# Hybrid encoder layer: the attention from the last query tile to the first with the mask written into the bias rows, and three pieces of work placed anew

## Chip, core and metric

The kernel runs on one core of a Trainium2 chip. The metric is the device time of one execution in microseconds (us). Engines are named as in the profile: PE (TensorE), DVE (VectorE), ACT (ScalarE), POOL (GpSimd), SP (SyncE, which here only issues DMAs).

## What is computed

One layer of a streaming encoder on x of 1024 tokens by 1024, in float32, with 256 memory tokens. Cut to what matters:

```python
proj = rms_norm(x, mix_pre_g) @ w_in                  # u (512) | q, k, v (8 heads x 64) | f_logit (8)
y_ssm = s5_mixer(u, ...)                              # complex diagonal SSM, gelu, gated linear unit
# forgetting attention, by query blocks of 128:
s = einsum(q_blk, k[:k_end]) * scale
s = where(q_pos >= k_pos, s + cum_log_f[q] - cum_log_f[k], -1e30)
y_fox = softmax(s) @ v[:k_end]
x = x + rms_norm(concat(rms_norm(y_ssm), rms_norm(y_fox)) @ w_out)
x = x + rms_norm(memory_cross_attention(rms_norm(x), mem_n, wq, wkv, wo))   # 4 heads
x = x + rms_norm((silu(h @ w_gate) * (h @ w_up)) @ w_down)                  # h = rms_norm(x), 2816 hidden
```

## The kernel before

**Number format.** Nearly every product is made of three matmuls (`mm3`, lines 122 to 124): each operand is split into a high and a low part (`split`: ACT writes the high part, L113, and DVE the rest, L115), and high x high, high x low and low x high are summed in PSUM.

**Stages.** In this order, by the times of the profiled execution: the input projection with the SSM (to about 232 us; its output product and gelu, L647 to L649, at 188 to 220); the forgetting attention, whose gaps PE fills with projections of the branch behind it (232 to 474); the output projection with the first value weights of the cross-attention between its products (474 to 545); the cross-attention (to 772); the FFN's gate and up products (772 to 1183); its down product (to the end).

**What sets the order.** The program is written as generators that are interleaved, and a scheduler with a cost table of its own then sets the order of every engine; `tc.high_priority` and `tc.issue_after` bend it. Tiles come from pools: 16 slabs of 8 KB a partition (`slab`), tags of smaller tiles (a 2 buffers, b 2, c 3, d 1, e 1, t2 3, yt 2), 3 split weight slabs (`whl`), 4 PSUM banks (`g`) and 2 score tiles of two banks each (`s`). A tile that is to be written waits until the last reader of its buffer is done.

**SSM output.** T holds the Toeplitz part in four quarters, for two halves s_ and two pairs of blocks. The first quarter lies in tile e; before, three more in two slabs, loaded by SP from T_d (L636). `ssm_out` makes, per half, four blocks of eight matmuls in a PSUM bank each, and ACT puts each through the gelu (L649, with one load of the activation table ahead). L318 is ACT's evacuation of the value projection, stored to v_d by POOL (L321); L299 and L300 are POOL's stores of q and k to qk_d.

**Attention.** For each of 8 heads and 8 query tiles of 128, `scores(h, t)` makes q k^T for the (t+1) x 128 keys up to the diagonal in a score tile s (L735, L736; and L738, a product of an identity and a triangle of large values that is added to the diagonal block). DVE adds the head's decay row ncb, broadcast to 128 partitions, and takes the minimum (L742; the signs are turned), ACT takes the exponential (L744), DVE scales (L745, L746). `turn` transposes the result on PE (L763) into slabs `pts`; `values` multiplies pairs of tiles with v (L777). Scores run two tiles ahead of `turn`. `prepare(h)` loads q, k and ncb of a head; it is called one head ahead. At the end `token_sums` adds up squares on PE by one-column matmuls (L239).

**Value weights.** `value_weights(h)` loads a head's values from kv_d (L1052), splits them into vh and vl, and multiplies them with wo (tiles t2 as weights against `whl`); heads 0 and 1 are stepped through between the output projection's products (`step(between)`), heads 2 and 3 follow.

**FFN.** Gate and up are done for pairs of hidden tiles by a scheme of seven products in place of eight (`gate_up`, `sums`; L1313 is every matmul of it, L1334 an addition of a bank to a kept tile, u2 one of these). `hid_sums(i)` makes four sums of a finished pair on DVE (L1371) and stores them (L1361, POOL). `wd_sums(k)` makes sums of the down weights on POOL (L1386) and stores them.

## Time and profile before

| | |
|---|---|
| median of 3 runs | 1402.24 us (1399.69 to 1403.91) |
| the profiled execution | 1403.55 us, span 1401.8 us, mean granted clock 0.996 |
| PE busy | 1373.7 us, 7149 matmuls |
| DVE, ACT, POOL busy | 973.7, 646.2, 377.3 us |
| moved by DMA | 242.03 MB, 173 GB/s in the mean |

How the lines read: a group is *line engine operation out<-in xcount | busy, mean ns | idle before it, releaser*; a timeline row is *start, duration, engine line operation out<-in xcount [idle before <-releaser]*; a wait is *engine, tile, line <- what it waited for: us in total, times, longest*. Matmuls are pipelined, so that the distance from one start to the next, not the duration, is what a matmul costs.

### The profile page before, as it was taken

The page shows a single profiled execution, that of the slowest core. Times are in us where ns is not written, and L with a number is a line of the kernel's source. Part 1 is how long each engine was busy: PE and PEld are TensorE (multiplying, and loading weights), DVE is VectorE, ACT ScalarE, POOL GpSimd, SP SyncE. Part 2 cuts the span into 40 slices and gives each one's busy share as a digit, 9 for nine tenths or more (in the row PEclk, how much of TensorE's full clock was granted, in tenths as well). Part 3 has the DMA queues.
Part 4 walks back from the last instruction along what each step waited for, and adds up shares of the span by engine and source line. Part 5 has one row for each costly group of instructions (what it writes and reads, how often), then busy time and mean ns, then how long its engine had stood idle before and what let it go on. Part 6 is the DMA issues. An engine that isn't in the chain of part 4 may idle for free.

```text
span 1401.8 us, 19885 instructions
## 1 busy us (share of the span) xinstructions
PE 1373.7 (98%) x7149; PEld 1144.9 (82%) x7149; DVE 973.7 (69%) x1740; ACT 646.2 (46%) x1262; POOL 377.3 (27%) x430
## 2 busy tenths in 40 slices
PE   9999999999999999999999999999999999999997
PEld 7889888879978777888888778888888888888886
DVE  7959954858667678445567998787777676655566
ACT  7373345866456547433344533333333334544441
POOL 0011110001111142001111466687666651000021
PEclk9999999999999999999999999999999999999999
DMA  6435765358662865035366354555444447965544
GB/s 218 141 105 165 216 222 139 83 155 252 184 194 83 222 194 186 0 105 169 131 219 233 135 180 157 189 188 173 160 141 163 153 151 245 355 195 195 180 166 165
DMA packets 104626, 242.03 MB, mean 173 GB/s; under 512 B 11528, under 2 KB 40200, under 8 KB 104336
## 3 DMA queue, kind: packets, MB, share of 16 engines
q1 hardware_dynamic: 86000, 178.86, 40.8%
q0 software_dynamic: 18528, 61.91, 12.4%
q8 instruction: 56, 0.92, 0.3%
q14 instruction: 42, 0.34, 0.1%
HBM read 172.05 MB, written 79.43 MB: 179 GB/s over the span
## 4 chain that ended last, share of the span: by engine, by line
PE 57%; DVE 2%; issue 1%; DMA 1%; POOL 0%; ACT 0%; DVEq 0%; SPq 0%; POOLq 0%; ACTq 0%
PE x L1313 15%; PE g L1313 12%; PE x L1591 7%; PE g L1591 7%; PE g L124 2%; PE g L122 2%; PE g L123 2%; PE x L122 2%; PE x L123 2%; PE x L124 2%; PE g L1109 1%; DVE op L115 1%; PE g L1220 0%; DVE ev L1371 0%; DMA slab<-in_w_gate 0%
## 5 line engine op out<-in xcount | busy, mean ns | idle before, releaser
L1313 PE MATMUL x<-slab,op 128*128 128x512 f32 x984 | 233.4, 389 | 0.0
L1313 PEld LDWEIGHTS x<-slab,op 128*128 128x128 f32 x984 | 184.7, 188 | 38.7 <-DVE op L115 0.5
L1313 PE MATMUL g<-slab,op 128*128 128x512 f32 x756 | 182.2, 390 | 2.3 <-DVE ev L1334 2.0
L115 DVE TENSOR_TENSOR slab<-slab 128x1024 fp32r<-128x1024 f32 (+2 forms) x96 | 115.0, 1208 | 82.9 <-ACT slab L113 81.2
L1313 PEld LDWEIGHTS g<-slab,op 128*128 128x128 f32 x756 | 141.6, 188 | 32.9 <-DVE ev L1334 2.4
L122 PE MATMUL g<-slab,whl 128*128 128x512 f32 (+1 forms) x416 | 151.7, 365 | 0.8 <-ACT slab L487 0.4
L123 PE MATMUL g<-slab,whl 128*128 128x512 f32 (+1 forms) x416 | 148.4, 357 | 0.0
L124 PE MATMUL g<-slab,whl 128*128 128x512 f32 (+1 forms) x416 | 148.4, 357 | 0.0
L113 ACT ACTIVATE slab<-slab 128x1024 fp32r<-128x1024 f32 (+2 forms) x96 | 99.0, 1037 | 102.4 <-DMA slab<-hs_d 75.2
L1591 PE MATMUL g<-slab 128*128 128x512 f32 x462 | 126.6, 389 | 0.0
L1591 PE MATMUL x<-slab 128*128 128x512 f32 x462 | 126.6, 389 | 0.0
L115 DVE TENSOR_TENSOR op<-slab,op 128x512 fp32r<-128x512 f32 x82 | 99.4, 1222 | 11.9 <-ACT op L113 11.5
L1591 PEld LDWEIGHTS g<-slab 128*128 128x128 f32 x462 | 86.7, 188 | 18.0
L1591 PEld LDWEIGHTS x<-slab 128*128 128x128 f32 x462 | 86.7, 188 | 18.0
L1386 POOL TENSOR_TENSOR wt<-wt 128x256 f32<-128x256 f32 x88 | 85.7, 974 | 30.6 <-DMA wt<-in_w_down 27.3
L113 ACT ACTIVATE op<-ss 128x512 fp32r<-128x512 f32 x63 | 39.5, 629 | 106.7 <-PE g L1313 50.9
L122 PEld LDWEIGHTS g<-slab,whl 128*128 128x128 f32 x416 | 78.7, 189 | 12.2 <-ACT whl L113 0.6
L124 PEld LDWEIGHTS g<-slab,whl 128*128 128x128 f32 x416 | 78.5, 189 | 11.6 <-DVE whl L115 0.2
L123 PEld LDWEIGHTS g<-slab,whl 128*128 128x128 f32 x416 | 78.7, 189 | 10.6
L113 ACT ACTIVATE op<-slab 128x512 fp32r<-128x512 f32 x82 | 51.1, 627 | 78.4 <-PE x L1313 40.8
L115 DVE TENSOR_TENSOR whl<-raw,whl 128x1024 fp32r<-128x1024 f32 (+2 forms) x58 | 66.0, 1144 | 20.8 <-ACT whl L113 20.5
L1416 POOL TENSOR_TENSOR ss<-slab 128x512 f32<-128x512 f32 x40 | 60.8, 1520 | 62.7 <-DMA slab<-in_w_gate 22.2
(397 smaller groups left out, 2876.2 us busy)
## 6 DMA issues: line engine op xcount, KB each, us to landing
hs_d<-ev POOLq DMA_DIRECT2D x77, 256.0 KB, 2.6
slab<-hs_d SPq DMA_DIRECT2D x35, 512.0 KB, 3.9
slab<-in_w_up SPq DMA_DIRECT2D x22, 512.0 KB, 4.4
wt<-in_w_down SPq DMA_DIRECT2D x44, 256.0 KB, 3.3
wt_d<-wt POOLq DMA_DIRECT2D x22, 512.0 KB, 3.8
slab<-in_w_gate SPq DMA_DIRECT2D x20, 512.0 KB
slab<-wt_d SPq DMA_DIRECT2D x20, 512.0 KB, 8.6
wd_d<-in_w_down SPq DMA_DIRECT2D x33, 256.0 KB, 4.7
```

The source lines that it names most:

```text
L113: first = act.activation(out=hi, in_=src, func=AF.Copy, scale=1.0 if mul is None else mul)
L115: (lo_eng or dve).tensor_tensor(out=lo, in0=src, in1=hi.bitcast(F32), op=ALU.subtract)
L122: pe.matmul(ps, lh, rh, start=first, stop=False)
L123: pe.matmul(ps, lh, rl, start=False, stop=False)
L124: pe.matmul(ps, ll, rh, start=False, stop=last)
L1109: pe.transpose(tp[:, k], src[:, (k0 + k) * P:(k0 + k + 1) * P], ident)
L1313: pe.matmul(ps, x[:, k], y[:, k], start=first and k + n == 0, stop=k == 3 and n == 2, skip_group_check=not first)
L1386: pool.tensor_tensor(out=o, in0=x, in1=y, op=ALU.subtract)
L1416: made[0] = pool.tensor_tensor(out=o, in0=x, in1=y, op=fn)
L1591: pe.matmul(banks[n][j], xo[:, u, js], wo[:, v], start=ends[0] and k == 0, stop=ends[1] and k == 2, skip_group_check=onto is not None)
```

## The change

The kernel is changed in four places.

1. The mask. The bf16 identity and triangle and their 64 matmuls go. `causal(h, t)` is new: POOL writes the large value in place into the diagonal block of the head's ncb tile. Since a tile's masked block must be plain for all later tiles, the query tiles of a head run from 7 to 0; each L742 of tile t is followed by `causal(h, t - 1)`, and `prepare` ends with `causal(h, 7)`. Slabs, value products, loads and the next head's `prepare` take the matching places.
2. T's two slabs become one slab and a tile of tag d, for the last quarter.
3. The split values of head 2 lie in one tile of tag a rather than two of t2; one empty step is put between heads 0 and 1.
4. `hid_sums(0)` is called behind u2 of the next `gate_up`, and each `wd_sums` from the second on one step later.

```diff
-    identb = const.tile([P, P], BF16, name="identb")
-    dve.tensor_copy(identb, ident)
-    maskb = const.tile([P, P], BF16, name="maskb")
-    pool.memset(maskb, 0.0)
-    pool.affine_select(out=maskb, in_=maskb, pattern=[[-1, P]], compare_op=ALU.is_ge,
-                       fill=-NEG, base=0, channel_multiplier=1)
...
-        full = [None] + [slab([P, 16, P], F32) for _ in range(2)]
-        T = [[tq, full[1][:, 0:8]], [full[2][:, 0:8], full[2][:, 8:16]]]
+        mid, tl = slab([P, 16, P], F32), tt("d", [P, 8, P])
+        T = [[tq, mid[:, 0:8]], [mid[:, 8:16], tl]]
...
+            causal(h, NT - 1)
+
+        def causal(h, t):
+            c = heads[h][2][:, t * P:(t + 1) * P]
+            pool.affine_select(out=c, in_=c, pattern=[[-1, P]], compare_op=ALU.is_ge, fill=-NEG,
+                               base=0, channel_multiplier=1)
...
-                dg = c1 == ke
                 pe.matmul(ps[:, c0:c1], qt, ka[:, 0, c0:c1], start=True, stop=False)
-                pe.matmul(ps[:, c0:c1], qt, ka[:, 1, c0:c1], start=False, stop=not dg)
-                if dg:
-                    pe.matmul(ps[:, ke - P:ke], identb, maskb, start=False, stop=True)
+                pe.matmul(ps[:, c0:c1], qt, ka[:, 1, c0:c1], start=False, stop=True)
...
                                      scalar=3e38, op0=ALU.add, op1=ALU.min, accum_out=nm)
+            if t:
+                causal(h, t - 1)
...
-            if t in (0, 2, 6):
+            if t in (3, 5, 7):
                 p = slab([P, 8, 256], F32)
-                if t == 0:
+                if t == 5:
...
-            if qc == 0:
+            if qc == 3:
                 yf.append(slab([P, 2, S]))
...
-        seq = [(h, t) for h in range(NH) for t in range(NT)]
+        seq = [(h, t) for h in range(NH) for t in reversed(range(NT))]
...
-                if t == 1 and h + 1 < NH:
+                if t == 6 and h + 1 < NH:
                     prepare(h + 1)
-                if (h, t) == (3, 5):
+                if (h, t) == (3, 2):
                     load_v(1)
...
-                if t % 2 and h % 2:
+                if t % 2 == 0 and h % 2:
                     values(h // 2, t // 2)
...
     def value_weights(h):
-        vh, vl = t2t([P, 2, 256], F32R), t2t([P, 2, 256], F32R)
+        if h == 2:
+            both = tt("a", [P, 2, 2, 256], F32R)
+            vh, vl = both[:, 0], both[:, 1]
+        else:
+            vh, vl = t2t([P, 2, 256], F32R), t2t([P, 2, 256], F32R)
...
     def first_values():
-        for h in range(2):
-            yield from value_weights(h)
+        yield from value_weights(0)
+        yield
+        yield from value_weights(1)
...
-    def gate_up(i, m, w, q):
+    def gate_up(i, m, w, q, behind_u2=None):
...
         u2 = q.add(2, p1)
+        if behind_u2:
+            behind_u2()
...
-            hid_sums(i)
+            if i:
+                hid_sums(i)
...
-    wd_sums(1)
     for n, (i, m) in enumerate(seq):
         if n + 1 < len(seq):
             ws[seq[n + 1]] = operands(*seq[n + 1])
-        gate_up(i, m, ws.pop((i, m)), Products(i, m))
-        wd_sums(n + 2)
+        gate_up(i, m, ws.pop((i, m)), Products(i, m), (lambda: hid_sums(0)) if n == 0 else None)
+        wd_sums(n + 1)
+    wd_sums(len(seq) + 1)
```

The order on the engines moves with it, in three places that matter below. First ACT around the SSM's first gelus, before and then after (L649 is L643 in the changed kernel, L318 is L312, L629 is L623):

```order
107 L318 ACTIVATE t_1991<-g,r_x 128x256
108 L629 ACTIVATE slab<-b 64x8x112 x2
109 L318 ACTIVATE t_2019<-g,r_x 128x256
110 L649 ACT_TABLE_LOAD
111 L649 ACTIVATE slab<-g 128x4x8x16 x4
112 L318 ACTIVATE t_2088<-g,r_x 128x256
```

```order
107 L312 ACTIVATE t_1984<-g,r_x 128x256
108 L623 ACTIVATE slab<-b 64x8x112 x2
109 L643 ACT_TABLE_LOAD
110 L643 ACTIVATE slab<-g 128x4x8x16 x4
111 L312 ACTIVATE t_2012<-g,r_x 128x256
112 L312 ACTIVATE t_2081<-g,r_x 128x256
```

The table load and the four gelus of the first half moved ahead of the evacuation of t_2012 (t_2019 before).

Second, POOL's queue at the same place, before and after (L724 is `causal`; qk_d and v_d are the stores of q, k and v):

```order
44 L299 DMA qk_d<-t_1946 128x512
45 L321 DMA v_d<-t_1991 128x256
46 L300 DMA qk_d<-a 128x1024
47 L321 DMA v_d<-t_2019 128x256
48 L321 DMA v_d<-t_2088 128x256
```

```order
42 L293 DMA qk_d<-t_1939 128x512
43 L315 DMA v_d<-t_1984 128x256
44 L724 AFFINE_SELECT b<-b 128x128
45 L294 DMA qk_d<-a 128x1024
46 L724 AFFINE_SELECT b<-b 128x128
47 L315 DMA v_d<-t_2012 128x256
48 L315 DMA v_d<-t_2081 128x256
```

The selects of tile 7 of heads 0 and 1 now stand between these stores; the other 62 follow through the attention, among POOL's stores.

Third, DVE in the FFN's first `gate_up`, before and after (op is an operand's low part, ev a kept tile or a sum; L1334 is L1338 in the changed kernel, L1371 is L1375, L115 is L109):

```order
1156 L115 TENSOR_TENSOR op<-ss,op 128x512
1157 L1371 TENSOR_TENSOR ev<-ev 128x512 x2
1158 L115 TENSOR_TENSOR op<-slab,op 128x512
1159 L1371 TENSOR_TENSOR ev<-ev 128x512 x2
1160 L1334 TENSOR_TENSOR ev<-g,ev 128x512
1161 L115 TENSOR_TENSOR op<-slab,op 128x512 x2
```

```order
1156 L109 TENSOR_TENSOR op<-slab,op 128x512 x2
1157 L1338 TENSOR_TENSOR ev<-g,ev 128x512
1158 L1375 TENSOR_TENSOR ev<-ev 128x512 x2
1159 L109 TENSOR_TENSOR op<-slab,op 128x512
1160 L1375 TENSOR_TENSOR ev<-ev 128x512
1161 L1338 TENSOR_TENSOR ev<-x,ev 128x512
1162 L1375 TENSOR_TENSOR ev<-ev 128x512
```

u2 moved ahead of the four sums, which now stand around the next L1338.

## The prediction

> **What bounds the kernel now.** I read the page's engine shares and its chain first, then the list of waits of TensorE (PE), then the timeline around the waits that the change touches, and last the stretches of the attention.
>
> ```profile
> PE 1373.7 (98%) x7149; PEld 1144.9 (82%) x7149; DVE 973.7 (69%) x1740; ACT 646.2 (46%) x1262; POOL 377.3 (27%) x430
> ...
> PE 57%; DVE 2%; issue 1%; DMA 1%; POOL 0%; ACT 0%; DVEq 0%; SPq 0%; POOLq 0%; ACTq 0%
> ```
>
> PE is busy for 1373.7 of 1401.8 us and carries the chain of work that ended last; no other engine reaches 70%. So only two things can shorten the run: PE work that goes, and time in which PE stands or runs slowly. The waits that the edits touch are these (us in total, times, longest):
>
> ```profile
> PE g L647 <- ACT t L318: 3.2, 1, 3.2
> PE s L735 <- DVE nlr L742: 2.4, 3, 0.9
> PE g L1313 <- DVE ev L1334: 2.0, 1, 2.0
> PE g L124 <- DVE t L115: 1.9, 2, 1.4
> ```
>
> L647 is the SSM's output product, L735 the scores, L1313 the FFN, L124 with tile t the split values.
>
> **Part 1: T's last quarter (lines 631 to 636).** Timeline of PE, and of ACT, around the first wait:
>
> ```profile
> 193.69 0.36 PE L123 MATMUL g<-whl,slab 128*128 128x256 f32 x1
> ...
> 196.40 0.28 PE L124 MATMUL g<-whl,slab 128*128 128x256 f32 x1
> 199.85 0.70 PE L647 MATMUL g<-slab 128*128 128x128 f32 x2 [3.17 <-ACT t L318]
> 200.34 0.63 PE L648 MATMUL g<-slab 128*128 128x128 f32 x2
> ...
> 202.90 0.63 PE L648 MATMUL g<-slab 128*128 128x128 f32 x2
> 203.80 0.39 PE L122 MATMUL g<-whl,slab 128*128 128x256 f32 x1 [0.27 <-ACT slab L649]
> ```
>
> ```profile
> 190.91 1.91 ACT L629 ACTIVATE slab<-b 64x896 f32<-64x896 f32 x2
> 199.32 0.47 ACT L318 ACTIVATE t<-g,r_x 128x256 f32<-128x256 f32 x1 [6.50 <-DMA qk_d<-t]
> 199.81 1.28 ACT L649 ACT_TABLE_LOAD   x1
> 203.15 1.57 ACT L649 ACTIVATE slab<-g 128x512 f32<-128x512 f32 x3 [2.05 <-PE g L647]
> ```
>
> ```profile
> 200.00:203.40 3.40, 3.40 (x16) 3.24 (x16) 0.00 (x0) 1.35 (x2) 0.54 (x1) 0.50 1.02 417
> ...
> 281.90:285.30 3.40, 3.40 (x10) 2.64 (x9) 1.70 (x7) 2.39 (x4) 0.85 (x2) 0.50 0.55 147
> ```
>
> The last block of the SSM's first half (b = 3) needs a PSUM bank. That bank is freed by L318, L318 needs a tile whose store is still under way (6.50 us of idle on ACT, released by the DMA), and behind L318 stand the table load and all four gelus. PE stands 3.17 us; then the stretch 200.00 to 203.40 runs at a granted clock of 0.50 (the number ahead of the DMA share), and a further 0.27 us goes at 203.80. The price: from 196.40 to 203.80 are 7.40 us. From 200.34 to 202.90 twelve matmuls take 2.56 us, 0.21 each at half clock, so 0.11 at full clock; the sixteen of the block plus one matmul ahead would take some 1.9 us. Lost: 5.5 us.
>
> In the new order of ACT the table load and the gelus stand ahead of that L318, and block 3 on PE follows block 2 at once; its bank now comes from the gelu of block 0. ACT is free at 190.91 + 1.91 = 192.82; with the table load (1.28) and one gelu (1.57/3 = 0.52) it is done at 194.62, and PE has finished block 2 at about 193.69. So PE waits 0.9 us instead, and I take 1.0. The second half's two quarter loads now lie apart, one of them earlier; the last quarter is not needed before the third block of that second half. **Term: -4.5 us** (5.5 less 1.0). Ends: -5.5 if the wait vanishes, 0 if it only moves.
>
> [...]
>
> ```profile
> 278.02 1.90 PE L239 MATMUL g<-ones,d 128*128 128x1 f32 x16
> ...
> 281.52 0.50 PE L122 MATMUL g<-whl,slab 128*128 128x512 f32 x1 [0.58 <-ACT slab L768]
> ```
>
> So by this row thin work followed by a short wait is enough to bring 3.4 us of half clock, which costs about 1.7 us of work. [...] Where the one-column sums stand closer together (L239 at the end of the attention, all eight in one row in the new order against six and two), it could come again: I keep +1.7 for the bounds.
>
> **Part 2: the mask.** 64 matmuls of L738 go. Their busy time of 14.7 us is not what they cost, since matmuls overlap; the distance from the start of one to the next start is:
>
> ```profile
> L738 PE MATMUL s<-maskb,identb 128*128 128x128 bf16 x64 | 14.7, 230 | 0.0
> ...
> 336.93 0.23 PE L738 MATMUL s<-maskb,identb 128*128 128x128 bf16 x1
> 337.00 0.72 PE L763 MATMUL g<-ident,c 128*128 128x128 f32 x5
> ...
> 441.62 0.23 PE L738 MATMUL s<-maskb,identb 128*128 128x128 bf16 x1
> 441.66 0.42 PE L735 MATMUL s<-slab,a 128*128 128x384 f32 x1
> ```
>
> 0.07 and 0.04 us; at 0.065, nearer to the commoner one, 64 make **-4.2 us** (ends -2.6 and -4.5). All of it is on the path, for PE has no other slack there.
>
> What comes is 64 selects on POOL, 128x128 in f32. The trace has one of just that form (the identity). The second and third rows are stretches of the attention (busy us of PE, PEld, DVE, ACT, POOL; then clock, DMA share, GB/s), and then loads (KB, median us to landing):
>
> ```profile
> masks.py:199 POOL TENSOR_SCALAR_AFFINE_SELECT ident<-ident 128x128 f32<-128x128 f32 x1 | 0.3, 293 | 0.0
> ...
> 290.00:320.00 30.00, 30.00 (x195) 23.71 (x194) 19.79 (x55) 21.28 (x49) 2.16 (x4) 1.00 0.56 163
> ...
> 440.00:470.00 30.00, 27.27 (x207) 23.16 (x207) 26.66 (x63) 23.65 (x52) 2.35 (x3) 1.00 0.58 171
> ...
> slab<-qk_d SPq DMA_DIRECT2D x16, 512.0 KB, 9.4
> ...
> a<-qk_d SPq DMA_DIRECT2D x16, 256.0 KB, 4.6
> ...
> slab<-wof_d SPq DMA_DIRECT2D x4, 512.0 KB, 9.7
> ```
>
> 64 x 0.293 = 18.8 us on POOL, which has 2 of 30 us to do: the work itself is hidden. The new thing is order. DVE's L742 of tile t writes the scores; only then may POOL mask tile t-1, and only then may DVE go on to L742 of t-1. The attention runs from about 232 to 474 us, so a query tile has 242/64 = 3.8 us of PE, and DVE some two thirds of it to fill; a select of 0.3 us between two L742 fits, with other DVE work in between, as long as POOL is free. It isn't always: the select of the next head's tile 7 waits for the load of nc_d (512 KB, no median of its own; its neighbours take 4.6 and 9.4 us), and the running head's next select stands behind it. In the new order that next one is wanted one to two tiles after the load is issued, 3.8 to 7.6 us. So POOL blocks between nothing and 9.4 - 3.8 = 5.6 us a head; PE has two score tiles ahead, which covers 3.8 of it. What can reach PE is 0 to 1.8 us for each of seven heads, 0 to 12.6 in all. The loads of 4.6 are covered and only few are as slow as 9.4: I take **+1.5 us**.
>
> At the start, the first two POOL selects wait for nc_d as well, with a store of qk_d and one of v_d behind them on POOL's queue; their readers stand several stores and loads further on in the queues of SP and ACT, so I cost them at nothing (rival b has the case that it is not). The attention begins with its largest tile rather than its smallest, where 2.4 us of waits for L742 stand already; and it ends on the smallest, with less PE work between the last values and the output product, whose last weight slab (wof_d, 9.7 us to landing) is now issued only some twenty matmuls, about 5 us, before its use (three matmuls take 0.96 us in part 4). Those ends, 0 to +4 at the tail and -2 to 0 from stalls at the head and the half clock at 281.90, I set together at **-0.5 us**.
>
> **Part 3: the split values.** PE's stalls, and the load behind them:
>
> ```profile
> 511.02 0.50 PE L122 MATMUL g<-whl,t 128*128 128x512 f32 x1 [0.24 <-ACT t L113]
> ...
> 514.52 0.73 PE L124 MATMUL g<-whl,t 128*128 128x512 f32 x2 [1.36 <-DVE t L115]
> ...
> 536.12 0.50 PE L122 MATMUL g<-whl,t 128*128 128x512 f32 x1 [0.69 <-ACT t L113]
> ...
> 538.29 0.74 PE L124 MATMUL g<-whl,t 128*128 128x512 f32 x2 [0.51 <-DVE t L115]
> ...
> t<-kv_d SPq DMA_DIRECT2D x4, 256.0 KB, 4.0
> ```
>
> 0.24 + 1.36 + 0.69 + 0.51 = 2.8 us. A head's split values take two of the tag's three buffers, so a head can't be split before the one ahead of it has been read: the first two waits are head 1's, the last two head 2's, whose matmuls follow head 1's at once. With head 2 in a tile of tag a its split needs nothing of head 1; and in the new order head 0's 24 matmuls stand in a row, with 72 others between them and head 1. Late next may be head 2's second weight slab: its split on ACT and DVE now stands close ahead of its use, its buffer being head 1's. I leave 0.8 us for it: **-2.0 us**, ends -2.8 and 0.
>
> **Part 4: the FFN.** Timeline of DVE, then PE's wait:
>
> ```profile
> 818.21 2.92 DVE L1371 TENSOR_TENSOR ev<-ev 128x512 f32<-128x512 f32 x2
> ...
> 821.65 2.92 DVE L1371 TENSOR_TENSOR ev<-ev 128x512 f32<-128x512 f32 x2
> 824.49 0.68 DVE L1334 TENSOR_TENSOR ev<-g,ev 128x512 f32<-128x512 f32 x1
> ...
> 825.23 0.96 PE L1313 MATMUL g<-slab,op 128*128 128x512 f32 x3 [2.00 <-DVE ev L1334]
> ```
>
> u2 (L1334) stands behind four sums of 5.8 us on DVE; in the new order it stands ahead of them, so the 2.00 us go. Two of the four sums stand ahead of the following L1334 on DVE, and that one is wanted a product later; L1371 feeds stores only, so I see no new wait of size. wd_sums move by one step each on POOL, DVE and SP; what they make is read in the last product, after the loop, so they cost nothing while POOL, 27% busy, keeps up. **Term: -2.0 us**, ends -2.0 and 0.
>
> [...]
>
> **Sum:** -4.5 - 4.2 + 1.5 - 0.5 - 2.0 - 2.0 = -11.7 us. The profiled execution took 1403.55 us (span 1401.8), so 1391.85; it lies 1.3 us above the median of the runs shown, 1402.24, so **1390.5 us**, 0.8% faster. The measurement can tell about 0.3% (4.2 us) from no change.
>
> **Rivals.** (a) *The chain DVE, POOL, DVE becomes the bound of the attention.* If PE waits in every tile for the select and the hand-overs around it, as it does for L742 three times now, each tile costs 0.3 to 0.5 us in place of the 1.5 us in all: 64 x 0.4 = 25.6, so 1390.5 - 1.5 + 25.6 = 1414.6 us, slower. It is slower than before from (11.7 + 1.5)/64 = 0.21 us a tile, and by over 0.3% from 0.27. For it speak DVE's 26.66 of 30 us in the last stretch and the three waits for L742; against it that PE is busy all of 290 to 320 while DVE has 10 us free. [...] (b) *The stall at 199.85 only moves:* the selects that wait for nc_d on POOL hold up stores, an L318 waits for a store, and the next bank comes no sooner. Then part 1 gives nothing: 1395.0. For it, ACT's 6.50 us were a DMA's; against it, block 3 no longer needs that bank. (c) *The tail of the attention pays:* the last weight slab late (+2.5, about half of 9.7 less 5) and the one-column sums in one row with the half clock that followed them before (+1.7): 1394.7. (d) *PE is held by DVE in the attention, so the mask matmuls were hidden:* -4.2 is lost, 1394.7. Against it, the stretch with PE at 30.00 of 30.
>
> **Numbers.** Forecast 0.55; (a) 0.06, half of it slower than before by over 0.3%; (b) 0.12; (c) 0.17; (d) 0.10. Two of (b), (c) and (d) together give 1399. The best ends of the terms, -5.5 - 4.5 + 0 - 2.0 - 2.8 - 2.0 = -16.8, give 1385.4. The range is 1384.5 to 1399. The line of 0.3% lies at 1398.0: (a) and pairs of the others cross it, so faster 0.85, within 0.3% 0.11, slower 0.04.
>
> **What would show it.** Right: no wait over 1.5 us at the SSM's block 3 and a clock of 1.00 around it; no rows of the mask on PE; selects of about 0.3 us; no L1313 wait for L1334; split values without a wait over 0.5 us; DVE's L742 rarely released by POOL. Wrong: PE's scores waiting for L742 in most heads for over 1 us, L742 waiting for a select behind a late nc_d; a new half-clock stretch between 455 and 475; the output product waiting for its last slab.

## The result, and the profile after

The changed kernel takes 1424.86 us (median of 5 runs, 1424.03 to 1428.54) against 1402.24 of the kernel before in the same runs: a ratio of 1.017 (95% interval 1.0149 to 1.019), 22.6 us slower. The forecast was 1390.5 us (1384.5 to 1399), so it was wrong, and in its sign. The profiled execution takes 1424.07 us (span 1422.3, mean granted clock 0.988), 20.5 us more than the one before.

Busy time, instructions, and shares of the chain that ended last, from the page of the changed kernel:

```profile
PE 1377.8 (97%) x7085; PEld 1148.4 (81%) x7085; DVE 977.6 (69%) x1739; ACT 647.1 (45%) x1262; POOL 399.7 (28%) x492
...
PE 56%; DVE 2%; issue 1%; POOL 0%; DMA 0%; ACT 0%; SPq 0%; DVEq 0%; POOLq 0%
```

PE has 64 matmuls fewer (7149 before) and yet 4.1 us more of busy time: some of its work ran slower. PE is still the bound, and the loss is time in which it stood or ran at half clock. Its waits (tile, line <- what it waited for: us in total, times, longest; L116 to L118 are the three matmuls of a product, L107 and L109 the two halves of `split` on ACT and DVE):

```profile
PE g L116 <- ACT a L107: 6.2, 1, 6.2
PE g L1317 <- DVE ev L1338: 5.5, 1, 5.5
PE g L116 <- ACT slab L767: 2.5, 2, 2.0
PE s L734 <- DVE nlr L739: 2.3, 3, 1.5
PE x L116 <- ACT slab L107: 2.1, 1, 2.1
PE g L762 <- DVE c L745: 1.8, 2, 1.0
PE g L117 <- DVE whl L109: 1.8, 1, 1.8
```

Two waits of 6.2 and 5.5 us stand where the longest was 3.2; the first stands in the value weights (part 3), the second in the FFN (part 4), the two places that were to give 2.0 us each.

**Where the 20.5 us arose.** Five stages, cut at the first matmul of the scores, of the output product, of the cross-attention's keys, and of the FFN. *Half clock* is half of the time that PE worked while 0.50 was granted (from the clock's record and PE's rows; the run's last 40 us left out; from one 128x512 matmul to the next are 0.43 us at 0.50, 545.23 to 545.66 in the changed kernel, and 0.23 at 1.00, 536.65 to 536.88); the stages stand without it. All in us, of the profiled executions. A profile is one execution, and the half clock differs from one to the next: below, the profiles of runs 1, 3, 5, 7, 11 and 13 are the shortest of their executions, those of runs 4, 8, 12, 14 and 15 the longest.

| | to scores (A) | attention (B) | output, value weights (C) | cross-attention (D) | FFN (E) | half clock | span |
|---|---|---|---|---|---|---|---|
| before | 230.5 | 238.6 | 70.1 | 216.0 | 643.2 | 3.4 | 1401.8 |
| after | 227.4 | 239.1 | 83.1 | 215.1 | 646.7 | 10.9 | 1422.3 |
| difference | -3.1 | +0.5 | +13.0 | -0.9 | +3.5 | +7.5 | +20.5 |

**A, part 1.** Timeline of PE at the SSM's block 3, then the stretch with that wait and the one behind it (length; busy us of PE, PEld, DVE, ACT, POOL; granted clock, DMA share, GB/s):

```profile
194.48 0.49 PE L641 MATMUL g<-slab 128*128 128x128 f32 x2 [0.78 <-ACT slab L643]
```

```profile
193.00:196.40 3.40, 2.62 (x24) 2.43 (x23) 0.00 (x0) 2.40 (x4) 0.00 (x0) 1.00 1.01 296
196.40:199.80 3.40, 3.40 (x31) 3.40 (x30) 0.00 (x0) 1.07 (x2) 0.84 (x2) 1.00 1.04 415
```

0.78 us of wait in place of 3.17, and no half clock.

**B, the attention.** The selects, and DVE's decay addition with what it waited for:

```profile
L739 DVE CUSTOM_DVE_ANT_0 c<-s,b 128x1024 f32<-128x1024 f32 (+3 forms) x64 | 48.1, 752 | 15.9 <-PE g L762 7.9 <-PE s L735 4.5 <-POOL b L724 3.1
L724 POOL TENSOR_SCALAR_AFFINE_SELECT b<-b 128x128 f32<-128x128 f32 x64 | 26.9, 423 | 113.3 <-DVE nlr L739 49.9 <-DMA b<-nc_d 31.7 <-DVE nlr L744 31.6
```

DVE waited for selects 3.1 us in the whole attention: the chain of rival (a) did not become the bound. The end of the attention, on ACT and then on PE:

```profile
468.73 1.06 ACT L107 ACTIVATE slab<-slab 128x1024 fp32r<-128x1024 f32 x1 [4.06 <-DMA slab<-wof_d]
469.69 0.46 ACT L107 ACTIVATE slab<-g,gains 128x256 fp32r<-128x256 f32 x1
```

```profile
469.84 1.90 PE L116 MATMUL x<-slab 128*128 128x512 f32 x4 [2.07 <-ACT slab L107]
```

The output product waits 2.07 us for the split of the first wof_d slab, issued at 460.40 and split at 468.73; the last slab, the one of rival (c), had not even been issued (478.48, next rows). The twelve profiles with descending tiles all have such a wait, of 0.39 to 2.41 us, the longest in run 12, where all four slabs are issued by 465.7; the five with ascending tiles have none. So it comes with the new end of the attention and not with the late last slab.

**C, the output product and value weights.** SP's queue in the changed kernel; then the same loads before:

```profile
460.40 18.40 SPq L1042 DMA_DIRECT2D slab<-wof_d  x4
478.84 0.43 SPq L1086 DMA_DIRECT2D e<-in_x  x1
...
492.11 0.33 SPq L957 DMA_DIRECT2D d<-in_post_g  x1
...
514.32 1.23 SPq L1083 DMA_DIRECT2D a<-t_d  x2
...
533.33 0.38 SPq L1055 DMA_DIRECT2D a<-kv_d  x1
```

```profile
458.36 6.38 SPq L1043 DMA_DIRECT2D slab<-wof_d  x3
...
471.73 0.32 SPq L1043 DMA_DIRECT2D slab<-wof_d  x1
472.10 0.42 SPq L1082 DMA_DIRECT2D e<-in_x  x1
...
487.74 0.33 SPq L958 DMA_DIRECT2D d<-in_post_g  x1
...
504.25 1.23 SPq L1079 DMA_DIRECT2D a<-t_d  x2
```

The row of four slabs ends with the fourth, at 460.40 + 18.40 = 478.80, where before it ended at 471.73 + 0.32 = 472.05: SP waited 16.8 us for PE's last work of the attention before it could issue it. The loads behind it on SP follow late: e<-in_x 6.7 us later, the gains (L957) 4.4, the next a<-t_d 10.1, although the output product began 2.6 us sooner (469.84 against 472.48). For the fourth slab itself PE waits nowhere: its split starts at 481.69, and the product that reads it follows at 484.77 without a wait. Then part 3's place, on DVE, ACT and PE:

```profile
532.02 1.28 DVE L1101 SCALAR_TENSOR_TENSOR e<-a,r,e 128x1024 f32<-128x1024 f32 x1 [2.55 <-DMA e<-in_x]
```

```profile
543.96 0.63 ACT L107 ACTIVATE a<-a 128x512 fp32r<-128x512 f32 x1 [5.75 <-DMA a<-kv_d]
```

```profile
544.64 0.80 PE L116 MATMUL g<-whl,a 128*128 128x512 f32 x1 [6.24 <-ACT a L107]
...
548.73 1.22 PE L116 MATMUL g<-whl,a 128*128 128x512 f32 x2 [1.16 <-ACT whl L107]
551.75 0.80 PE L117 MATMUL g<-whl,a 128*128 128x512 f32 x1 [1.80 <-DVE whl L109]
```

Head 2's values now need a tile of tag a. That tag's two buffers carry the output product's a tiles, and the load (533.33) follows the last reader of one, L1101, which itself had waited 2.55 us for a late in_x. ACT has it 10.6 us after its issue, and PE stands 6.24 us. Then the second weight slab is late, as the forecast feared, by 1.16 + 1.80 us and not 0.8.

**E, the FFN.** PE, DVE and POOL around u2 (L1338):

```profile
828.06 2.88 PE L1317 MATMUL g<-slab,op 128*128 128x512 f32 x12
830.78 5.38 PE L1317 MATMUL x<-slab,op 128*128 128x512 f32 x23
841.68 4.57 PE L1317 MATMUL g<-slab,op 128*128 128x512 f32 x11 [5.53 <-DVE ev L1338]
```

```profile
830.82 0.68 DVE L1360 TENSOR_TENSOR ev<-ev 128x512 f32<-128x512 f32 x1
...
832.01 4.15 DVE L1360 TENSOR_TENSOR ev<-ev 128x512 f32<-128x512 f32 x1
836.09 2.07 DVE L109 TENSOR_TENSOR op<-slab,op 128x512 fp32r<-128x512 f32 x1
...
840.95 0.68 DVE L1338 TENSOR_TENSOR ev<-g,ev 128x512 f32<-128x512 f32 x1
841.55 1.28 DVE L1375 TENSOR_TENSOR ev<-ev 128x512 f32<-128x512 f32 x2
```

```profile
832.38 1.30 POOL L1420 TENSOR_TENSOR ss<-slab 128x512 f32<-128x512 f32 x1
833.62 0.74 POOL L1390 TENSOR_TENSOR wt<-wt 128x256 f32<-128x256 f32 x1
834.32 1.29 POOL L1420 TENSOR_TENSOR slab<-slab 128x512 f32<-128x512 f32 x1
```

u2 does stand ahead of the sums (L1375) on DVE. But PE comes to it sooner: between the product that u2 reads (828.06) and the next one in its bank (841.68) lie only 23 matmuls on record; in the kernel before it were 45. And a multiplication (L1360) that takes 0.68 us in its other row takes 4.15 where POOL works at three operations in a row.

### The profile page after: what moved, and what is told of

Read it like the earlier page. It is cut to its first block, busy times and chain, and to the rows that moved or that the text cites. A ratio compares the mean times of both kernels' runs of the same rounds, so it can differ in the third digit from the quotient of the medians.

```text
span 1422.3 us, 19938 instructions
## 1 busy us (share of the span) xinstructions
PE 1377.8 (97%) x7085; PEld 1148.4 (81%) x7085; DVE 977.6 (69%) x1739; ACT 647.1 (45%) x1262; POOL 399.7 (28%) x492
## 4 chain that ended last, share of the span: by engine, by line
PE 56%; DVE 2%; issue 1%; POOL 0%; DMA 0%; ACT 0%; SPq 0%; DVEq 0%; POOLq 0%
PE x L1317 15%; PE g L1317 12%; PE x L1598 7%; PE g L1598 7%; PE g L118 2%; PE g L116 2%; PE g L117 2%; PE x L117 2%; PE x L118 2%; PE x L116 2%; PE g L1113 1%; DVE op L109 1%; PE g L1224 0%; DMA wt<-in_w_down 0%; DVE ev L1360 0%
## 5 line engine op out<-in xcount | busy, mean ns | idle before, releaser
L109 DVE TENSOR_TENSOR slab<-slab 128x1024 fp32r<-128x1024 f32 (+2 forms) x96 | 115.7, 1214 | 88.9 <-ACT slab L107 87.0
L116 PE MATMUL g<-slab,whl 128*128 128x512 f32 (+1 forms) x416 | 151.1, 363 | 0.8 <-ACT slab L481 0.4
L118 PE MATMUL g<-slab,whl 128*128 128x512 f32 (+1 forms) x416 | 148.2, 357 | 0.0
L107 ACT ACTIVATE slab<-slab 128x1024 fp32r<-128x1024 f32 (+2 forms) x96 | 99.1, 1037 | 106.0 <-DMA slab<-hs_d 79.6
L109 DVE TENSOR_TENSOR op<-slab,op 128x512 fp32r<-128x512 f32 x82 | 95.2, 1172 | 10.0 <-ACT op L107 9.8
L116 PEld LDWEIGHTS g<-slab,whl 128*128 128x128 f32 x416 | 78.5, 189 | 12.0 <-ACT whl L107 0.6
L107 ACT ACTIVATE op<-slab 128x512 fp32r<-128x512 f32 x82 | 51.2, 628 | 80.3 <-PE x L1317 40.0
L118 PEld LDWEIGHTS g<-slab,whl 128*128 128x128 f32 x416 | 78.4, 189 | 11.5 <-DVE whl L109 0.2
L117 PEld LDWEIGHTS g<-slab,whl 128*128 128x128 f32 x416 | 78.5, 189 | 10.6
L107 ACT ACTIVATE op<-ss 128x512 fp32r<-128x512 f32 x63 | 39.6, 630 | 103.3 <-PE g L1317 57.6
L109 DVE TENSOR_TENSOR whl<-raw,whl 128x1024 fp32r<-128x1024 f32 (+2 forms) x58 | 65.3, 1132 | 23.2 <-ACT whl L107 22.9
L116 PE MATMUL g<-whl,slab 128*128 128x512 f32 (+2 forms) x224 | 74.8, 345 | 4.1 <-ACT slab L767 2.0
```

Of the source, the lines that this page charges most:

```text
L107: first = act.activation(out=hi, in_=src, func=AF.Copy, scale=1.0 if mul is None else mul)
L109: (lo_eng or dve).tensor_tensor(out=lo, in0=src, in1=hi.bitcast(F32), op=ALU.subtract)
L116: pe.matmul(ps, lh, rh, start=first, stop=False)
L117: pe.matmul(ps, lh, rl, start=False, stop=False)
L118: pe.matmul(ps, ll, rh, start=False, stop=last)
```

## The experiments

The theory after the first comparison: three separate losses, each of a part: (1) the fourth wof_d slab falls free late, since tile pairs 0 and 2 share a slab and pair 2's is read early and pair 0's last, and SP's queue stands behind its load; (2) part 3's tile of tag a, or its empty step; (3) the moved sums of the FFN. The rivals: the selects or the new direction of the attention cost the time; the late loads alone cause all three; each loss is only the half clock behind some other wait. The runs, with the stages as above (ratios to the kernel before in the same runs):

| run | ratio, 95% | A | B | C | E | half clock |
|---|---|---|---|---|---|---|
| 1 loads not held | 1.0139, 1.0116 to 1.0163 | 226.4 | 238.9 | 82.0 | 646.7 | 8.6 |
| 2 split values back | 1.0113, 1.0093 to 1.0133 | 226.6 | 240.9 | 78.8 | 646.7 | 8.1 |
| 3 FFN back | 1.0146, 1.0129 to 1.0163 | 227.1 | 237.9 | 84.0 | 645.2 | 11.2 |
| 4 mask matmuls back | 1.0160, 1.0144 to 1.0177 | 226.6 | 242.1 | 83.5 | 646.8 | 11.8 |
| 5 slab shared otherwise | 1.0096, 1.0067 to 1.0126 | 225.8 | 238.8 | 76.3 | 646.8 | 4.7 |
| 6 = 5, parts 3 and 4 back | 1.0025, 1.0006 to 1.0044 | 227.0 | 238.6 | 68.9 | 645.1 | 5.1 |
| 7 part 1 alone | 0.9992, 0.9971 to 1.0012 | 226.3 | 239.6 | 68.9 | 645.3 | 1.7 |
| 8 parts 1, 3, 4 | 1.0088, 1.0058 to 1.0118 | 226.9 | 239.5 | 77.1 | 646.8 | 13.3 |
| 9 = 5, hid_sums back | 1.0070, 1.0049 to 1.0091 | 226.4 | 239.3 | 75.1 | 645.1 | 9.1 |
| 10 = 5, wd_sums back | 1.0105, 1.0076 to 1.0134 | 226.9 | 239.2 | 76.5 | 646.7 | 10.1 |
| 11 = 5, tag a back | 1.0061, 1.0038 to 1.0084 | 226.1 | 238.9 | 73.1 | 646.8 | 7.4 |
| 12 = 5, empty step back | 1.0084, 1.0063 to 1.0105 | 227.1 | 239.4 | 72.3 | 646.6 | 10.8 |
| 13 = 6 without a mask | 1.0018, 0.9997 to 1.0039 | 227.3 | 238.8 | 69.3 | 645.2 | 1.7 |
| 14 = 7 without a mask | 1.0003, 0.9986 to 1.0021 | 227.8 | 236.9 | 69.4 | 645.2 | 10.6 |
| 15 = 7, hid_sums moved | 1.0011, 0.9994 to 1.0028 | 227.6 | 240.0 | 70.0 | 646.7 | 5.9 |

D is 213.9 to 216.0 in all of them.

**Run 1: the loads behind the fourth slab no longer wait for it.**

```diff
-        wo_read = sp.dma_start(out=w, in_=wof_d[i])
+        dma = sp.dma_start(out=w, in_=wof_d[i])
+        wo_read = dma if i < 3 else wo_read
```

> The changed kernel with one edge moved: the loads of the output projection's rows and of x wait for the third weight slab of w_out (wof_d) rather than the fourth. In the changed kernel SP stands from 461.4 to 478.5 us before the fourth slab's load, with all these loads behind it, 6.7 us later than before. Theory S (SP is held by the fourth slab, and what stands behind it is what costs): the stretch from the first output product to the first cross-attention product behind the value weights, 88.7 us in the changed kernel and 70.1 before, falls to 70 to 77, and the whole to 1407 to 1414 us. Rival V (it is the split values of head 2 in tag a, whose load waits for an output tile to be read): the stretch stays at 84 to 89 and the whole at 1420 to 1425.

1421.39 us, not the 1407 to 1414 expected. PE now waits 6.6 us in one piece for the split of the fourth slab itself (of two such waits, the other is that for the first slab):

```profile
PE x L116 <- ACT slab L107: 8.6, 2, 6.6
```

The late slab costs much the same by either way, so freeing the queue alone cures nothing.

**Runs 2 and 3: part 3 undone, part 4 undone.** Two `t2` tiles and no empty step; `hid_sums(0)` and `wd_sums` at their old places.

```diff
-        yield from value_weights(0)
-        yield
-        yield from value_weights(1)
+        for h in range(2):
+            yield from value_weights(h)
```

> The changed kernel with part 3 undone (head 2's split values in two tiles of t2 again, no empty step). Rival V: the 6.2 us in which PE waits for ACT's split of a at 544.6 and the three half-clock stretches behind it go, the stretch falls from 88.7 to 70 to 76 and the whole to 1407 to 1413. Theory S: the loads are still late, the output loop still ends late, and at most the wait on tag a goes: stretch 79 to 88, whole 1415 to 1424.

```diff
-            if i:
-                hid_sums(i)
+            hid_sums(i)
...
```

> The changed kernel with part 4 undone (hid_sums(0) at the end of its pair, each wd_sums one step earlier, as before). Theory F (part 4 put POOL's sums of the down weights ahead of its operand sums, so that DVE comes late to u2): PE's wait of 5.5 us for u2 and the two half-clock stretches go, the old 2.0 us come back, the FFN takes 5.4 us less and the whole is 1418 to 1421 us. Rival F' (the wait hangs on when POOL and DVE meet, not on the edit): 1423 to 1428 and the wait stays over 4 us.

1419.12 and 1423.77 us, against 1424.86 of the changed kernel: run 2 is clearly faster, run 3's lead lies within the intervals. Neither gains what was expected where its part was the whole cause (1407 to 1413, and 1418 to 1421). Run 3's u2 wait is 2.8 us and its E 1.5 us shorter. While the slab is late, undoing part 3 shows other late loads instead (a wait of 2.8 us for DVE's L1088), so these two runs alone don't price the parts.

**Run 4: the mask's matmuls back, the descending order kept, no selects.**

```diff
...
+                if dg:
+                    pe.matmul(ps[:, ke - P:ke], identb, maskb, start=False, stop=True)
...
-            if t:
-                causal(h, t - 1)
```

> The changed kernel with descending query tiles, but with the mask as 64 bf16 matmuls again and no selects on POOL. Rival P (the chain DVE, POOL, DVE and selects that wait for nc_d on POOL's queue hold PE up): the attention, 242.5 us from the first score to the first output product, falls by more than the matmuls' 4.2 us bring back: 236 to 242, and the whole is under 1424. Theory O (the order, not the selects: the selects cost PE at most 3 us): the matmuls come back with 4.2 us less what little the selects cost: attention 243 to 247, whole 1425 to 1430.

1425.63 us, no different from the changed kernel. So the selects are not what costs the 22 us.

**Run 5: pairs 0 and 1, which are read last, share a slab.**

```diff
-                if t == 5:
-                    pts[h, 0], pts[h, 2] = p[:, 0:2], p[:, 2:8]
+                if t == 3:
+                    pts[h, 0], pts[h, 1] = p[:, 0:2], p[:, 2:6]
```

> The changed kernel with the attention's slabs shared otherwise: the transposed weights of the query pairs 0 and 1 of a head share a slab, and pair 2 has its own (in the changed kernel 0 and 2 share, so that with descending tiles a slab falls free only behind pairs 3 and 1). Theory S2 (the fourth weight slab of w_out is late because of these slabs, and SP or the last quarter of the output products waits for it): SP issues that load by 470 us, no x product waits for it, the stretch from the first output product to the first cross-attention key product falls from 88.7 to 72 to 80 us and the whole to 1408 to 1416. Rival V2 (part 3's tile of tag a is what costs, whenever the loads come): stretch over 82, whole over 1418.

1415.14 us: 0.74% of the 1.7% are gone. SP's rows of this run:

```profile
458.56 5.59 SPq L1042 DMA_DIRECT2D slab<-wof_d  x4
464.20 1.41 SPq L1086 DMA_DIRECT2D e<-in_x  x1
```

All four slabs are issued by 464.15, and the x waits of the output product are gone but for 0.39 us; PE's wait for tag a falls from 6.24 to 1.7 us with them. C is 6.8 us shorter, half clock 6.2 (in the shortest of its four executions; by the medians the kernel gains 9.7 in all). So the shared slab is shown as the cause of nearly half of the loss.

**Runs 6 and 7: what is left without parts 3 and 4** (run 5 with the edits of runs 2 and 3, `wd_sums` too), **and part 1 alone**, in the kernel before:

```diff
-        full = [None] + [slab([P, 16, P], F32) for _ in range(2)]
-        T = [[tq, full[1][:, 0:8]], [full[2][:, 0:8], full[2][:, 8:16]]]
+        mid, tl = slab([P, 16, P], F32), tt("d", [P, 8, P])
+        T = [[tq, mid[:, 0:8]], [mid[:, 8:16], tl]]
```

> The changed kernel with the slabs shared as in the run before it, and parts 3 and 4 undone: what is left is part 1 and the mask with descending tiles. Theory S2 with V and F (late slab, tag a and part 4 are all of the loss): stretch of the output products 69 to 74 us, FFN to the end 643 to 645 us, the whole 1396 to 1400 us. Rival H (the longer waits come from half-clock stretches and from meetings of POOL and DVE that any shift brings): stretch 74 to 82, FFN 646 to 650, whole 1402 to 1412.

> The kernel before with part 1 alone (T's last quarter in a tile of tag d). If a gain of 4.8 us at the SSM's first half stays to the end: 1396 to 1399 us, the FFN from its first product to the end 643 to 644 us. Rival H: it is eaten by a later stage, above all by a wait for u2 in the FFN with half clock behind it: 1400 to 1405 and FFN 646 to 649.

1404.58 and 1402.77 us (10 runs each), where 1396 to 1400 and 1396 to 1399 were expected if nothing else were lost. Run 6 is 0.71% faster than run 5: parts 3 and 4 cost some 10 us, and C is back at 68.9. Run 7 has A 4.2 us shorter, and the time is that of the kernel before all the same; E is 2.1 longer. Its FFN source is unchanged, but the scheduler set it in another order, and u2's wait is 2.8 us, not 2.0, with one of 0.9 us for an operand ahead of it:

```profile
PE g L1313 <- DVE ev L1334: 2.8, 1, 2.8
```

**Run 8: the attention as before, with parts 1, 3 and 4** (run 4's edit, and the tiles in their old order and places).

```diff
...
-        seq = [(h, t) for h in range(NH) for t in reversed(range(NT))]
+        seq = [(h, t) for h in range(NH) for t in range(NT)]
...
```

> The kernel before with parts 1, 3 and 4, the attention as before (ascending tiles, mask matmuls). If parts 3 and 4 are bad by themselves (V, F): output stretch 75 to 80 us, FFN 646 to 649, whole 1405 to 1412. If they were bad only behind late loads (S): output stretch 66 to 71, FFN 641 to 645, whole 1392 to 1399.

1414.91 us: C is 77.1, 7 us longer than before although no slab is late (the fourth is issued at 470.7, before at 471.7). Parts 3 and 4 lose without the attention's help.

**Runs 9 to 12: run 5 with one half of part 4 or of part 3 undone each** (`hid_sums`, run 3's edit; the empty step, run 2's; `wd_sums`; the tile of tag a).

```diff
+    wd_sums(1)
...
-        wd_sums(n + 1)
-    wd_sums(len(seq) + 1)
+        wd_sums(n + 2)
```

```diff
-        if h == 2:
-            both = tt("a", [P, 2, 2, 256], F32R)
-            vh, vl = both[:, 0], both[:, 1]
-        else:
-            vh, vl = t2t([P, 2, 256], F32R), t2t([P, 2, 256], F32R)
+        vh, vl = t2t([P, 2, 256], F32R), t2t([P, 2, 256], F32R)
```

> The kernel of the fifth run (slabs shared otherwise) with one half of part 4 undone: hid_sums(0) at the end of its pair again, wd_sums as changed. Theory F1 (moved sums let POOL run its operand sums without a store in between, and DVE's multiply L1360 ahead of u2 stands through three of them, 4.15 us): PE's wait for u2 falls from 5.7 to 2 to 3 us, FFN from its first product to the end from 648.3 to 644 to 647.5. Rival F2 (the later wd_sums are the cause): wait still 5.5 to 6, FFN 648 to 650.

> The kernel of the fifth run with the other half of part 4 undone: each wd_sums one step earlier again, hid_sums(0) behind u2. F1: wait for u2 5.5 to 6 us, FFN 648 to 650. F2: wait 2 to 3 us, FFN 644 to 647.5.

> The kernel of the fifth run with head 2's split values in two tiles of t2 again; the empty step between heads 0 and 1 stays. Theory V1 (the tile of tag a is the loss: its load waits on SP for an output tile to be read): the stretch from the first output product to the first key product falls from 77.8 to 69 to 73 us, whole 1402 to 1409. Rival V3 (the empty step is the loss: head 1's last products stand directly ahead of head 2's, so that the weight slab that head 2 needs is split too late): stretch 75 to 80.

> The kernel of the fifth run without the empty step between heads 0 and 1; head 2's split values stay in the tile of tag a. V1: stretch 75 to 82 us. V3: the waits of 2.1 and 2.3 us for the split weight slab (whl) go, stretch 68 to 73.

Against run 5's 1.0096: hid_sums back 1.0070 (u2's wait 2.8 us, E 1.7 us shorter), wd_sums back 1.0105 (5.7 us, nothing gained), tag a back 1.0061, the empty step back 1.0084. These ratios differ by no more than the intervals allow, so it is the waits and stages that tell them apart. The moved `hid_sums` is what lengthens u2's wait; the multiplication of 4.15 us ahead of it, which run 9 was to shorten, stays as it is in run 9. Of part 3 each half adds to C, 3.2 us the tile (run 11) and 4.0 the step (run 12), and each leaves another wait: with tag a undone (run 11; 75.0 us in C with its half clock, where 69 to 73 or 75 to 80 was expected) PE waits 5.5 us for a split of a t2 tile; with the step undone (run 12) 2.1 us for tag a's. With both undone (run 6) the wait for t2 is 0.5 us. The line of run 11, and that of run 12's wait for the first wof_d slab:

```profile
PE g L116 <- ACT t L107: 5.5, 1, 5.5
```

```profile
PE x L116 <- ACT slab L107: 2.4, 1, 2.4
```

Neither the tile alone nor the step alone explains part 3. In run 11 the t2 tile's load is issued at 534.30, with no wait of its own but behind a weight load (533.86) for which SP had waited 3.7 us, until DVE had split a weight slab: once more a load held by the one ahead of it on SP.

**Runs 13 and 14: no mask at all, descending and ascending** (run 6 without its selects, run 7 without its matmuls; of each the lines that go). Both leave the mask out of what is computed.

```diff
-            causal(h, NT - 1)
...
-            if t:
-                causal(h, t - 1)
```

```diff
-                if dg:
-                    pe.matmul(ps[:, ke - P:ke], identb, maskb, start=False, stop=True)
```

> The kernel of the sixth run (part 1, descending tiles, slabs shared otherwise, parts 3 and 4 as before) with neither selects nor mask matmuls: the mask is left out of the computation. If the selects cost PE what the 64 mask matmuls cost (theory K), the attention, 242.0 us with the selects, falls by 3 to 5 to 237 to 239. If the mask was hidden in the first place (theory D: PE is held by other waits in the attention, and saved work only lengthens them), it stays at 240.5 to 243.

> The kernel of the seventh run (before with part 1) without the 64 mask matmuls: the mask is left out of the computation, tiles ascend. K: the attention, 241.3 us with them, falls to 236 to 238, whole 3 to 5 us less than the seventh run's. D: 239.5 to 243.

1405.7 and 1404.7 us (10 runs each). In B: descending with selects 239.0 (median of the ten profiles that have them, 237.9 to 240.9), without 238.8, so the selects cost nothing that shows; what falls from 242.0 to 238.8 with the half clock in it is the half clock. Ascending without the matmuls 236.9, with them 239.5 to 240.0 (runs 7, 8, 15): they are worth 2.6 to 3.1 us (1.7 against the 238.6 of the kernel before, which lacks part 1); descending 242.1 with (run 4) and 238.8 without, 3.3. The descending order itself costs 1.9 (238.8 less 236.9) to 2.4 (242.1 less 239.7). And even run 14, which has nothing of the mask and keeps the order, is no faster than run 7, where 3 to 5 us were expected. Scores now wait in one place for 3.75 us (longest in run 7: 1.7),

```profile
397.61 0.79 PE L735 MATMUL s<-slab,a 128*128 128x512 f32 x1 [3.75 <-DVE nlr L740]
```

and six windows of 3.41 us in the attention ran at half clock (8.9 us lost there, run 7: 1.7; these two profiles lie at opposite ends of their executions). Over ten runs each the mean granted clock is 0.9928 against 0.9961, which is at most 4.6 us of 1400: about what the matmuls gave, the clock took.

**Run 15: run 7 with `hid_sums(0)` moved.**

```diff
+        if behind_u2:
+            behind_u2()
...
-            hid_sums(i)
+            if i:
+                hid_sums(i)
```

> The kernel of the seventh run (before with part 1) with hid_sums(0) moved behind u2, wd_sums as before. F1 in its present form (with the sums moved the scheduler also moves PE's products: 23 matmuls rather than 49 stand between the two products into u2's bank, so PE comes to it earlier than DVE does): wait for u2 5 to 6 us, FFN 648 to 650 against 645.3. Rival (it takes the late loads or part 3 as well): wait under 3 us, FFN 642 to 646.

1404.38 us; u2's wait is 5.7 us where run 7 has 2.8, and E 1.4 us longer (4.0 with half clock). In the median the difference of the two lies within the intervals.

```profile
PE g L1313 <- DVE ev L1334: 5.7, 1, 5.7
```

The order of the program shows the rest: with the sums in their old place 49 matmuls are on record between the product that u2 reads and the next one in its bank (runs 7 and 9), with the sums moved 23 (the changed kernel, and run 10). u2 comes earlier on DVE, and PE comes earlier still. In all ten profiles with moved `hid_sums` the wait is 5.5 to 5.7 us, in the other six changed ones 2.8.

## Why the prediction was wrong, step by step

- **Part 1 (-4.5): right.** The wait is 0.78 us (0.9 to 1.0 foretold); that the clock stays at 1.00 behind so short a wait was my estimate, and it did. Rival (b) did not come. With its half clock A fell by 4.8 (232.2 to 227.4), and by 4.4 to 6.4 in the other runs. It did not reach the total: in run 7's profile the attention and the FFN gave 1.0 and 2.1 us of it back; where the rest stays in its other runs is open.
- **The mask's matmuls (-4.2, ends -2.6 and -4.5):** 2.6 to 3.3 of the attention at full clock by runs 4, 7, 13 and 14, so rival (d), that they are hidden wholly, is false for the stage. In no whole time does it show (run 4 against the changed kernel, run 14 against run 7). The term took it that what PE saves the kernel saves; in run 14 it turned into a longer wait for DVE and into half clock.
- **The selects (+1.5): too much**, 0.2 or nothing by run 13. Three in four take the 0.29 us foretold; the rest, of up to 1.38, make the mean 0.42. DVE's 64 decay additions take 48.1 us, before 47.9, so the selects did not hold them up.
- **The ends of the attention (-0.5): wrong sign**, by 1.9 to 2.4 for the order alone, and the tail's wait and half clock on top. The tail (a wait of 2.07, and 3.41 us at half clock from 470.07) costs about what I had priced rival (c) at, +4.2, but that is luck: the wait is for the first weight slab and stands in runs whose last slab is early, and no half clock follows the attention's one-column sums (487.67).
- **The failed step for nearly half of the loss is the late last slab:** I priced it by the wait of the product that needs it, and left out what stands behind its load on SP. That product waits for nothing, and the loads behind come 4.4 to 10.1 us late (where they are let past, in run 1, the product waits 6.6). The slab's buffer falls free with pair 0, the last one; I had read from the order only that its issue comes twenty matmuls ahead of its use. Run 5 measures the choice at 0.74%, 10 us.
- **Part 3 (-2.0, ends -2.8 and 0): the sign was wrong**, +7 us in C by runs 5, 6 and 8. I counted the waits for the buffers that the change frees and not those for the buffer that it takes: tag a belonged to the output product's tiles, so the load of head 2's values went behind the last of them, and was in use 10.6 us after its issue where I had quoted a median of 4.0 to landing. That wait is partly the late slab's again: in run 5 it is 1.7 us.
- **Part 4 (-2.0, ends -2.0 and 0): the sign was wrong**, +1.5 us in E and half clock behind it. I read DVE's order and not PE's, which the scheduler changed along with it. The other 2.0 of E's +3.5 are not part 4's: run 7 has them too.
- **The half clock** had +1.7 in a bound. It is +7.5 in these two profiles.

## What to carry to other kernels

When a tile changes its tag or its partner in a slab, price the load that waits for the new buffer, and everything that stands behind that load on its queue, not only the reader that it serves. When an instruction moves ahead on one engine, read its partner engine's order as well: the scheduler moved both here, and an earlier reader turned a wait of 2.8 us into one of 5.7 (runs 7 and 15). On this kernel, with PE 98% busy, a wait of 2 us cost up to 1.7 more in half clock (3.41 us at 0.50 behind the 2.07 at the end of the attention), so a saving on PE counts only when the next supplier is not just behind it.

## What the runs showed of the hardware

**Half clock and the idle time of PE.** In each profile, the last 40 us left out, the stretches at 0.50 last 3.41 us or a multiple (the changed kernel's begin at 282.33, 394.97, 470.07, 541.75 and 838.70, all whole multiples of 3.413 us apart). On the grid that these beginnings give, windows of the changed kernel, and two of the kernel before around its 2.00 us wait for u2:

```profile
391.56:394.97 3.41, 1.43 (x8) 1.09 (x7) 2.09 (x5) 2.59 (x5) 0.39 (x2) 1.00 0.34 135
394.97:398.39 3.42, 3.42 (x11) 2.75 (x10) 3.42 (x6) 2.11 (x4) 0.84 (x2) 0.50 0.62 193
466.65:470.07 3.42, 1.35 (x11) 1.12 (x10) 0.25 (x1) 1.34 (x3) 0.00 (x0) 1.00 0.79 304
470.07:473.48 3.41, 3.41 (x9) 2.63 (x9) 3.41 (x5) 2.99 (x6) 0.71 (x1) 0.50 0.01 5
```

```profile
821.20:824.62 3.42, 2.02 (x9) 1.33 (x8) 3.39 (x4) 0.95 (x2) 3.01 (x4) 1.00 0.43 163
824.62:828.03 3.41, 2.80 (x12) 2.35 (x13) 3.41 (x3) 0.00 (x0) 3.15 (x4) 1.00 0.84 298
```

The windows of the changed kernel in which PE worked 1.43 and 1.35 us are each followed by one at half clock; the 2.00 us wait of the kernel before lies on both sides of an edge (824.62), and no half clock follows. Counted over the 17 profiles, each on its own grid (windows at full clock between 60 and 1380 us):

| PE idle in the window | windows | followed by half clock |
|---|---|---|
| under 1.0 us | 6248 | 0 |
| 1.0 to 1.4 | 57 | 1 |
| 1.4 to 1.93 | 36 | 11 |
| 1.93 or more | 40 | 40 |

Left out are the windows at 264 to 284 us, where the one-column sums stand: there one in each of 14 profiles is followed by half clock after less than 0.9 us of idle time (0.58 in the kernel before, 278.48 to 281.90), so idle time alone doesn't sort the windows of thin work. Of the 94 windows at half clock the 28 in which PE was idle for 0.65 us or more are followed by another, the other 66 by full clock. So a wait of 2 to 3 us cost 1.7 us more (half of 3.41 us of work) or nothing, by where it fell on the grid: the 2.8 us before u2 lie across an edge in runs 7 and 13 (at 820.1 and 821.3), and nothing follows; in runs 3, 6, 9 and 14 at least 2.5 of them lie in one window, and 3.41 us at half clock follow. Every window with 1.93 us of idle time or more was followed by half clock, and one with 1.17 was. Much of the scatter goes with the granted clock: run 13's ten executions go from 1400.12 us at a mean clock of 0.998 to 1408.59 at 0.991.

**A DVE row beside three of POOL.** The multiplication of 4.15 us (0.68 in its other row, at 830.82) begins 0.37 us ahead of three POOL operations in a row (832.38 to 834.32 + 1.29 = 835.61) and ends 0.55 us behind them, at 836.16. Beside the same three operations it takes 4.15 us in run 7 (0.35 us ahead, 0.56 behind) and 4.14 in run 10 (0.36 and 0.56). In all sixteen changed profiles, with part 4 or without, the multiplications of this line from 800 to 845 us take 1.49 to 1.84 us in the mean, in the kernel before 0.96. No run took POOL's operations away, so it is not shown that they are the cause.
